# The passage from the output projection to the squared-ReLU MLP: who forms the second column pair's sums, and which product comes when

## The chip, the cores and the metric

The kernel runs on one core of one Trainium2 chip (eight cores on two dies; the other seven are idle here). The metric is the device time of one execution in microseconds, the median of several runs. A profile of one execution stands beside it; its times are counted from the first instruction.

## The reference, cut to what matters

A prompt of 256 rows and a sample of 1024 rows, 1024 wide, go through one encoder layer in fp32: two attention branches, merged by gates, an output projection with a residual, then an RMSNorm and a squared-ReLU MLP with hidden width 4096, and a last RMSNorm. The end of the layer and the encoder are all that this change concerns:

```python
    x = x + merged @ w_out
    h = _rmsnorm(x, g_mlp)
    return x + jnp.square(jax.nn.relu(h @ w_up)) @ w_down
```

## The kernel before, in words

Each fp32 matmul is done as three products of a rounded high part and a residual low part: ScalarE makes the high part (`activation` Copy into fp32r), VectorE the low part by a subtraction (`split`, L184; `split_steps`, L308). `six` (L340) then issues low weight by high activation, high weight by low activation, high by high, for each of four or eight 128-deep slices.

`h @ w_up` and the product with `w_down` are done by Strassen's method in the form with seven products. The activations `h` of the sample (transposed) are cut in four blocks: A11 and A12 come from rows 0 to 511, A21 and A22 from rows 512 to 1023. Seven left factors are held split in SBUF for the whole of `h @ w_up`: A11, A12, A22 and the sums S1 = A21 + A22, S2 = S1 - A11, S3 = A11 - A21, S4 = A12 - S2. The raw sums are formed by VectorE in `combine` (L1361, in pieces, as a generator of twelve steps) and `combine_last` (L1379), and `halves` (L314) splits one factor in two halves of 128x1024.

The weights are taken 256 columns at a time, 16 pairs. `right_pair` (L367) is a generator: it issues the two loads of 512 KB on SyncE's queue, has GpSimd form the right sums `ta` and `tb` (four subtractions 128x512, L377 to L380), and then splits raw[0], ta, tb and raw[1] into `parts[0]` to `parts[3]`, one ScalarE and one VectorE step each. All these tiles take one of ten "w" buffers; activations take one of 33 "m" buffers. The first pair is prepared during the output projection.

`up(j, b, parts, hooks)` (L1693) does one pair. On TensorE, in order: A11 by parts[0] into a bank `x`, A12 by parts[0] into `y`, (for j > 0 the prompt's product with parts[0]), S2 by parts[1] added to `x`, S3 by parts[1] into `z`, S1 by parts[2] added to `x`, A22 by parts[2] added to `z`, S4 by parts[3] added to `x`, (for j = 0 the prompt's product with parts[0]), the prompt's product with parts[3]. One such product of the sample, `seven` (L357), is 12 matmuls of 512 columns; one of the prompt, `prompt` (L360), is 24 of 256 columns. Copies of `x` and `z` (`c1`, `c2`, `c7`, by ScalarE) are added by VectorE to later states of the banks (`relu2_sum`, L1689), which also squares the ReLU. The four blocks of the result are joined with the prompt's to `u` (128x640), GpSimd forms the four sums that the next Strassen product needs (L1743 to L1746), and SyncE's queue stores seven blocks of 320 KB (L1748). Every stage buffer (`u0` to `u6`, `c1`, `c2`, `c7`) exists once.

PSUM has eight banks under four tags: "mm" three, "sc" two, "pt" two, "pv" one. A new tile of a tag waits until an old one of the tag has been read.

From the second half of the output projection on (L1416) the order on each engine is the order of the program text (`manual_schedule` for all engines). Work of the passage is threaded into the first pair by `hooks`: `entering` (L1752) is a generator, and each `next(hooks)` in `up` issues its next piece. In the kernel before, the pieces after the successive products of the first pair are: splits of S3; the transposes of the last prompt row block (`turn_prompt(9)`, two banks "pt", copied out by ScalarE) and splits of S1; splits of A22; `combine_last` with the splits of S4; nothing; `split_prompt` (the prompt's activations, two halves). The generator `nb` of the next pair is moved by `steps_of(nb, 3)` (L1733) and by `steps_of(b, 2)` in the next call of `up`.

Of the kernel before, what the change touches and what calls it, by code (L numbers as in the profile page):

```python
# [11 lines left out]
F32R = mybir.dt.float32r  # L12
# [3 lines left out]
P = 128  # L16
# [81 lines left out]
def encoder_kernel(  # L98
# [229 lines left out]
    def turned(t, tags=("pt", "pt")):  # L328

        banks = []  # L330
        for h in range(2):
            ps = bank(tags[h], "tr")
            for i in range(4):
                k = 4 * h + i
                nc.tensor.transpose(ps[:, P * i : P * (i + 1)], xn[t][:, P * k : P * (k + 1)], ident)
            banks.append(ps.rearrange("p (i q) -> p i q", i=4))
        del xn[t]
        return banks
# [991 lines left out]
    hp_raw = {}  # L1330
    raws_h = {}

    def turn_prompt(t):

        if not hp_raw:
            for i in range(2):
                hp_raw[i] = slot("praw", (P, 4, NP))
        cols = slice(P * (t - 8), P * (t - 7))
        banks = turned(t)
        yield  # L1340
        for h in range(2):
            nc.scalar.activation(hp_raw[h][:, :, cols], banks[h], AF.Copy)
# [33 lines left out]

    combined = {}

    def combine_last():  # L1379
        s2, a12 = combined[S2], combined[S4]  # L1380
        for i in range(2):
            nc.vector.tensor_tensor(a12[i], a12[i], s2[i], op=ALU.subtract)
            act[S4][i] = slot("chi", (P, 2, 512), F32R), slot("clo", (P, 2, 512), F32R)
            split(*act[S4][i], a12[i])

    def right_up(j, out, make=wslot):
        return right_pair([w_up3[:, :, c : c + P] for c in (2 * P * j, 2 * P * j + P)], out, make)
# [1 line left out]
    with ExitStack() as pre:  # L1389
        late = pre.enter_context(tc.tile_pool(name="late", bufs=4))  # L1390

        def lslot(name, shape=(P, D), dt=F32):
            return late.tile(list(shape), dt, name=name, tag="l4", bufs=6)

        for i in (4, 5, 6):
            specs[n_out + i] = specs[n_out + i][:2] + (lslot,)
        gm = slot("gm2")
        nc.sync.dma_start(gm, g_mlp[0].partition_broadcast(P))
        xn = {}
        p0 = []  # L1400
        b0 = right_up(0, p0, slot)

        def ahead():

            yield from b0
            yield from halves(A11, raws_h[0, 0])
            yield from halves(A12, raws_h[0, 1])

        more, sums = ahead(), combine()
        for hh in range(2):  # L1410
            sl = slice(512 * hh, 512 * hh + 512)
            ws = [weight(0) for _ in range(4)]
            parts = {}
            if hh:

                ctx.enter_context(tc.manual_schedule(engines=ALL))  # L1416

            def part(t):
                if t >= NT:
                    return  # L1420
                n = 2 if hh else KC
                mhi = [qslot("mhi", (P, n, P), F32R) if hh else slot("mhi", (P, n, P), F32R) for _ in range(KC // n)]
                mlo = slot("mlo", (P, KC, P), F32R)
                for c in range(0, KC, 2):
                    split(mhi[c // n][:, c % n : c % n + 2, :], mlo[:, c : c + 2, :], mT.at(c, P * t, P, 2))
                parts[t] = [(mhi[k // n][:, k % n, :], mlo[:, k, :]) for k in range(KC)]

            part(0)
            part(1)
            for t in range(NT):  # L1430
                m = parts.pop(t)
                ps = bank("mm")
                run(mm3(ps, [(m[k], (ws[k // 2][0][:, k % 2, :], ws[k // 2][1][:, k % 2, :]))
                             for k in range(KC)]))
                if hh == 0:
                    nc.vector.tensor_tensor(x2[t][:, sl], x2[t][:, sl], ps, op=ALU.add)
                    part(t + 2)
                    if 2 <= t < 6:
                        prepare()
                    elif t in (6, 7):  # L1440
                        next(more)
                    continue
                turning = (turn_sample if t < 9 else turn_prompt)(t - 1) if t else iter(())
                next(turning, None)
                nc.vector.tensor_tensor(x2[t][:, sl], x2[t][:, sl], ps, op=ALU.add)
                xn[t] = slot("xn", (P, D))
                ss = small.tile([P, 1], F32, name="ss")
                nc.scalar.activation(xn[t], x2[t], AF.Square, accum_out=ss)
                sd = small.tile([P, 1], F32, name="sd")
                nc.scalar.activation(sd, ss, AF.Sqrt, bias=eps, scale=1.0 / D)  # L1450
                if 0 < t < 7:
                    next(more)
                steps_of(sums, (0, 1, 4)[max(t - 7, 0)])
                rs = small.tile([P, 1], F32, name="rs")
                nc.vector.reciprocal(rs, sd)
                nc.vector.scalar_tensor_tensor(xn[t], x2[t], rs, gm, op0=ALU.mult, op1=ALU.mult)
                nc.sync.dma_start(scr_x[t], x2[t])
                next(turning, None)
                part(t + 2)
                steps_of(more, (1, 1, 1, 1, 1, 3, 2, 0, 0, 0)[t])  # L1460
                steps_of(sums, (2, 3)[t - 7] if 6 < t < 9 else 0)
        run(halves(S2, combined[S2]))
        run(sums)
    narrow.close()


# [212 lines left out]
    with ExitStack() as pre:  # L1679
# [9 lines left out]
        def relu2_sum(out, ps, other):  # L1689
            nc.vector.tensor_tensor(out, ps, other, op=ALU.add)  # L1690
            nc.vector.scalar_tensor_tensor(out, out, 0.0, out, op0=ALU.max, op1=ALU.mult)

        def up(j, b, parts, hooks):  # L1693

            def prompt_out(ps, dst):
                for i, d in enumerate(dst):
                    relu2(d[:, 512:], ps[:, P * i : P * i + P])

            u = [stage(f"u{i}", TH) for i in range(7)]
            u11, u12, u22, u21 = u[A11], u[A12], u[A22], u[S3]  # L1700
            x, y, z = bank("mm", "x"), bank("pt", "y"), bank("sc", "z")
            nb = np_ = None
            seven(x, A11, parts[0], 0, last=False)
            c1 = stage("c1", 512)
            nc.scalar.activation(c1, x, AF.Copy)
            steps_of(b, 2)
            next(hooks, None)
            seven(y, A12, parts[0], 1)
            relu2_sum(u11[:, :512], y, c1)
            steps_of(b, 2)  # L1710
            if j:
                pa = prompt(parts[0])
            if j + 1 < FF // P // 2:
                np_ = []
                nb = right_up(j + 1, np_)
                next(nb)
            next(hooks, None)
            seven(x, S2, parts[1], 0, False, False)
            c2 = stage("c2", 512)
            nc.scalar.activation(c2, x, AF.Copy)  # L1720
            if j:
                prompt_out(pa, (u11, u21))
            steps_of(b, 2)
            next(hooks, None)
            seven(z, S3, parts[1], 1, last=False)
            c7 = stage("c7", 512)
            nc.scalar.activation(c7, z, AF.Copy)
            next(hooks, None)
            seven(x, S1, parts[2], 0, False, False)
            relu2_sum(u22[:, :512], x, c7)  # L1730
            next(hooks, None)
            if nb:
                steps_of(nb, 3)  # L1733
            seven(z, A22, parts[2], 1, False)
            relu2_sum(u21[:, :512], z, c2)
            next(hooks, None)
            seven(x, S4, parts[3], 1, False)
            relu2(u12[:, :512], x)
            next(hooks, None)
            if not j:  # L1740
                prompt_out(prompt(parts[0]), (u11, u21))
            prompt_out(prompt(parts[3]), (u12, u22))
            nc.gpsimd.tensor_tensor(u[S1], u21, u22, op=ALU.add)  # L1743
            nc.gpsimd.tensor_tensor(u[S2], u[S1], u11, op=ALU.subtract)
            nc.gpsimd.tensor_tensor(u[S3], u11, u21, op=ALU.subtract)
            nc.gpsimd.tensor_tensor(u[S4], u12, u[S2], op=ALU.subtract)  # L1746
            for i in (A11, S1, A22, S2, S3, A12, S4):
                nc.sync.dma_start(scr_u[j // 4][:, i, j % 4, :], u[i])  # L1748
            next(hooks, None)
            return nb, np_  # L1750

        def entering():  # L1752

            run(halves(S3, combined[S3]))
            yield
            run(turn_prompt(9))
            run(halves(S1, combined[S1]))
            yield
            run(halves(A22, combined[A22]))
            yield  # L1760
            combine_last()
            yield
            yield
            split_prompt()
            yield
# [32 lines left out]
```

## Time and profile before

| | |
|---|---|
| time, median of 3 runs | 1791.44 us (1791.1 to 1794.48) |
| span of the profiled execution | 1788.8 us |
| TensorE busy | 1731.5 us, 97% of the span |
| VectorE, ScalarE, GpSimd busy | 55%, 40%, 28% |
| granted TensorE clock, mean | 0.987 |
| output projection, second half, ends | at about 982 us |
| first pair's first product starts | at 982.66 us |
| third pair's first product starts | at 1048.50 us |

A row of the timeline gives start, duration, engine, line and operation, output and inputs; a bracket at its end is the time for which the engine stood idle before it and the instruction that, by the profile, released it. Where an instruction waited for several things, the name in the bracket can be that of another instruction of the same engine than the one that was really waited for. A matmul's duration includes its way through the array, so the rate is read from start to start. PE is TensorE, DVE VectorE, ACT ScalarE, POOL GpSimd, SPq SyncE's queue of DMA issues.

### The profile page before, as it was taken

The numbers are of one execution on the slowest core, as the hardware profiler recorded it, in microseconds if no ns is written. First come the engines' busy times: TensorE is split into PE (matmuls) and PEld (weight loads), VectorE is DVE, ScalarE is ACT, GpSimd is POOL, SyncE is SP. The second block draws the span as 40 slices with busy tenths as digits, with TensorE's granted clock in tenths as the row PEclk, the third lists the DMA queues.
The fourth block names the chain that finished last, engine by engine and source line by source line (L and its number), as shares of the span: only waits on it lengthen the run. The fifth ranks groups of instructions, "written<-read, shape, count | busy, mean of one in ns | idle before, by whom it ended". The sixth has DMA issues, their size and how long they took to land.

```text
span 1788.8 us, 25229 instructions
## 1 busy us (share of the span) xinstructions
PE 1731.5 (97%) x9248; PEld 1466.8 (82%) x9248; DVE 991.7 (55%) x1683; ACT 714.1 (40%) x1531; POOL 501.6 (28%) x396
## 2 busy tenths in 40 slices
PE   7999999999999999999999799999999999999998
PEld 6898888777777889878888688888888788888886
DVE  6623333345545466566737655454554876667575
ACT  6232223344444355454426533333333433333345
POOL 0222321223322111100010255565555451315050
PEclk9999999989999999999999899999999999999999
DMA  6415335555455853164411144433444854623333
GB/s 230 144 37 165 108 105 147 143 147 146 138 161 143 252 158 103 61 241 142 190 47 82 54 140 150 148 118 121 140 150 169 299 199 142 241 95 117 127 113 118
DMA packets 218067, 256.26 MB, mean 143 GB/s; under 512 B 21455, under 2 KB 148771, under 8 KB 217816
## 3 DMA queue, kind: packets, MB, share of 16 engines
q1 hardware_dynamic: 209512, 232.32, 40.4%
q0 software_dynamic: 7344, 20.24, 3.4%
q10 hardware_dynamic: 1088, 2.10, 0.3%
q8 instruction: 73, 1.20, 0.3%
q14 instruction: 50, 0.41, 0.1%
HBM read 169.10 MB, written 90.73 MB: 145 GB/s over the span
## 4 chain that ended last, share of the span: by engine, by line
PE 61%; DVE 3%; ACT 2%; DMA 2%; issue 1%; POOL 0%; SPq 0%; ACTq 0%; DVEq 0%; POOLq 0%
PE dn L344 20%; PE mm L192 13%; PE x L344 10%; PE pv L344 5%; PE z L344 5%; PE y L344 2%; PE pv L1053 2%; PE pt L1039 1%; PE sc L1016 1%; PE sc L1017 1%; PE mm L344 1%; DMA raw<-in_w_down_dram 0%; DVE ulo L186 0%; PE pv L538 0%; DMA raw<-in_w_in_dram 0%
## 5 line engine op out<-in xcount | busy, mean ns | idle before, releaser
L344 PE MATMUL x<-chi,wlo 128*128 128x512 f32 x424 | 172.1, 406 | 6.9 <-ACT phi L185 6.9
L344 PE MATMUL dn<-dhi,ulo 128*128 128x512 f32 x448 | 174.6, 390 | 2.8 <-DVE ulo L186 2.8
L344 PE MATMUL dn<-dhi,uhi 128*128 128x512 f32 x448 | 174.3, 389 | 0.0
L344 PE MATMUL dn<-dlo,uhi 128*128 128x512 f32 x448 | 174.3, 389 | 0.0
L344 PE MATMUL x<-clo,whi 128*128 128x512 f32 x424 | 168.5, 397 | 0.0
L344 PE MATMUL x<-chi,whi 128*128 128x512 f32 x424 | 167.9, 396 | 0.0
L377 POOL TENSOR_TENSOR tb<-raw 128x512 f32<-128x512 f32 x30 | 39.0, 1302 | 453.6 <-PE mm L192 139.6
L311 DVE TENSOR_TENSOR wlo<-ta,whi 128x1024 fp32r<-128x1024 f32 x30 | 56.6, 1887 | 184.7 <-ACT whi L309 184.7
L311 DVE TENSOR_TENSOR wlo<-raw,whi 128x1024 fp32r<-128x1024 f32 x60 | 92.4, 1540 | 105.7 <-ACT whi L309 105.7
L344 PEld LDWEIGHTS dn<-dhi,ulo 128*128 128x128 f32 x448 | 84.1, 188 | 21.4 <-DVE ulo L186 3.8
L344 PEld LDWEIGHTS x<-chi,wlo 128*128 128x128 f32 x424 | 81.8, 193 | 22.9 <-ACT phi L185 7.3
L186 DVE TENSOR_TENSOR ulo<-uraw,uhi 128x1024 fp32r<-128x1024 f32 x56 | 92.0, 1664 | 11.7 <-ACT uhi L185 11.7
L344 PEld LDWEIGHTS dn<-dlo,uhi 128*128 128x128 f32 x448 | 84.1, 188 | 17.4
L344 PEld LDWEIGHTS dn<-dhi,uhi 128*128 128x128 f32 x448 | 84.1, 188 | 17.4
L344 PEld LDWEIGHTS x<-chi,whi 128*128 128x128 f32 x424 | 81.4, 192 | 17.9
L515 ACT ACTIVATE s<-s,o 128x128 f32<-128x128 f32 (+1 forms) x120 | 52.4, 437 | 103.8 <-DVE o L513 55.2
L344 PEld LDWEIGHTS x<-clo,whi 128*128 128x128 f32 x424 | 81.9, 193 | 14.5
L1515 POOL TENSOR_TENSOR t<-raw,t 128x1024 f32<-128x1024 f32 x16 | 47.1, 2959 | 143.3 <-DMA raw<-in_w_down_dram 143.3
L1666 DVE TENSOR_TENSOR v<-v,dn 128x512 f32<-128x512 f32 x90 | 59.6, 683 | 42.6 <-PE dn L344 38.5
L344 PE MATMUL dn<-dhi,up 128*128 128x512 f32 x224 | 73.5, 389 | 0.0
L344 PE MATMUL pv<-phi,wlo 128*128 128x256 f32 x256 | 72.4, 283 | 0.9 <-ACT u L1686 0.9
L344 PE MATMUL z<-chi,wlo 128*128 128x512 f32 x184 | 72.7, 395 | 0.0
(326 smaller groups left out, 4753.0 us busy)
## 6 DMA issues: line engine op xcount, KB each, us to landing
scr_u<-u SPq DMA_DIRECT2D x112, 320.0 KB
uraw<-scr_u SPq DMA_DIRECT2D x56, 512.0 KB
raw<-in_w_in_dram SPq DMA_DIRECT2D x33, 512.0 KB
raw<-in_w_up_dram SPq DMA_DIRECT2D x32, 512.0 KB
raw<-in_w_down_dram SPq DMA_DIRECT2D x28, 512.0 KB
sg<-scr_g SPq DMA_DIRECT2D x32, 256.0 KB
uraw<-scr_u SPq DMA_DIRECT2D x28, 256.0 KB
v<-scr_v SPq DMA_DIRECT2D x96, 64.0 KB
```

Source lines behind the costliest of these rows:

```text
L186: nc.vector.tensor_tensor(lo, src, hi.bitcast(F32), op=ALU.subtract)
L192: nc.tensor.matmul(ps, a, b, start=i == 0, stop=i == len(seq) - 1)
L311: nc.vector.tensor_tensor(lo, src, hi.bitcast(F32), op=ALU.subtract)
L344: nc.tensor.matmul(ps, a, b, start=first and i == 0, stop=last and i == len(seq) - 1, skip_group_check=True)
L377: nc.gpsimd.tensor_tensor(tb[:, 0], b12, b11, op=ALU.subtract)
L515: nc.scalar.activation(s[:, h, :W], s[:, h, :W], AF.Exp, bias=nm[:, h : h + 1], accum_out=l[:, h : h + 1])
L1016: nc.tensor.matmul(ps[:, :W], q, st["k"][1][:, P * lo : P * lo + W], start=True, stop=False)
L1017: nc.tensor.matmul(ps[:, :W], q, st["k"][0][:, P * lo : P * lo + W], start=False, stop=True)
L1039: nc.tensor.transpose(ps[:, P * (i % 4) : P * (i % 4) + P], s[:, h, P * b : P * b + P], ident)
L1053: nc.tensor.matmul(pv[:, HD * h : HD * h + HD], pt[:, 2 * b + h, :], src, start=b == 0, stop=b == W // P - 1)
L1515: nc.gpsimd.tensor_tensor(o, a, b, op=ALU.subtract)
L1666: nc.vector.tensor_tensor(v, v, ps, op=ALU.add)
```

## The change

In the call for the first pair (j = 0):

- the bank `y` comes from "sc" instead of "pt";
- the second pair's right sums come from a new generator `second_pair`, where VectorE forms `ta` and `tb`, and raw[0] is split before them (in the order raw[0], sums, ta, the last sum and tb, raw[1]);
- after the first pair's product A22, a new function `first_two` does the second pair's products A11 and A12 (banks "mm" and "pt", copy in the buffer "c7"), ahead of the first pair's last product S4; the second call of `up` takes them over and begins with the prompt's product;
- VectorE's sums of `y` and `z` (`u11`, `u21`) of the first pair come after `first_two`;
- the prompt's product with parts[3] goes to a bank "mm" instead of "pv";
- the four joins of `u` are made by VectorE instead of GpSimd.

In `entering`, the splits of S1 move one piece later, and S4's difference is made in two halves: the first right behind the transposes of the last prompt block, the second, with both splits of S4, after the product A22. At the end of the output projection the last two steps of `combine` come before the splits of S2. In the call for j = 1, `u11`'s sum comes after `c2`. Pairs from the third on are as before.

```diff
-    def combine_last():
+    def combine_last(i):
         s2, a12 = combined[S2], combined[S4]
+        nc.vector.tensor_tensor(a12[i], a12[i], s2[i], op=ALU.subtract)
+
+    def second_pair(out):
+
+        raw = [wslot("raw", (P, KC, P)) for _ in range(2)]
         for i in range(2):
-            nc.vector.tensor_tensor(a12[i], a12[i], s2[i], op=ALU.subtract)
-            act[S4][i] = slot("chi", (P, 2, 512), F32R), slot("clo", (P, 2, 512), F32R)
-            split(*act[S4][i], a12[i])
+            nc.sync.dma_start(raw[i], w_up3[:, :, P * (2 + i) : P * (3 + i)])
+        yield
+
+        def parts(src):
+            out.append((wslot("whi", src.shape, F32R), wslot("wlo", src.shape, F32R)))
+            return split_steps(*out[-1], src)
+
+        yield from parts(raw[0])
+        b11, b21, b12, b22 = raw[0][:, :4], raw[0][:, 4:], raw[1][:, :4], raw[1][:, 4:]
+        ta, tb = wslot("ta", (P, 2, 4, P)), wslot("tb", (P, 2, 4, P))
+        nc.vector.tensor_tensor(tb[:, 0], b12, b11, op=ALU.subtract)
+        nc.vector.tensor_tensor(ta[:, 1], b22, b12, op=ALU.subtract)
+        nc.vector.tensor_tensor(ta[:, 0], b22, tb[:, 0], op=ALU.subtract)
+        yield
+        yield from parts(ta)
+        nc.vector.tensor_tensor(tb[:, 1], b21, ta[:, 0], op=ALU.subtract)
+        yield from parts(tb)
+        yield from parts(raw[1])
...
+        run(sums)
         run(halves(S2, combined[S2]))
-        run(sums)
...
+        def first_two(j, parts):
+
+            x, y = bank("mm", "x"), bank("pt", "y")
+            seven(x, A11, parts[0], 0, last=False)
+            c1 = stage("c7", 512)
+            nc.scalar.activation(c1, x, AF.Copy)
+            seven(y, A12, parts[0], 1)
+            opened[j] = x, y, c1
...
-            x, y, z = bank("mm", "x"), bank("pt", "y"), bank("sc", "z")
...
+            if j == 1:
+                x, y, c1 = opened.pop(j)
+                z = bank("sc", "z")
+            else:
+                x, y, z = bank("mm", "x"), bank("pt" if j else "sc", "y"), bank("sc", "z")
...
+            if j > 1:
+                relu2_sum(u11[:, :512], y, c1)
...
-                nb = right_up(j + 1, np_)
+                nb = right_up(j + 1, np_) if j else second_pair(np_)
...
             nc.scalar.activation(c2, x, AF.Copy)
+            if j == 1:
+                relu2_sum(u11[:, :512], y, c1)
...
             seven(x, S1, parts[2], 0, False, False)
+            if not j:
+                steps_of(nb, 2)
             relu2_sum(u22[:, :512], x, c7)
             next(hooks, None)
-            if nb:
+            if j and nb:
                 steps_of(nb, 3)
             seven(z, A22, parts[2], 1, False)
-            relu2_sum(u21[:, :512], z, c2)
+            if j:
+                relu2_sum(u21[:, :512], z, c2)
             next(hooks, None)
+            if not j:
+                first_two(1, np_)
+                next(hooks, None)
+                relu2_sum(u11[:, :512], y, c1)
+                relu2_sum(u21[:, :512], z, c2)
             seven(x, S4, parts[3], 1, False)
             relu2(u12[:, :512], x)
             next(hooks, None)
             if not j:
+                steps_of(nb, 1)
                 prompt_out(prompt(parts[0]), (u11, u21))
-            prompt_out(prompt(parts[3]), (u12, u22))
-            nc.gpsimd.tensor_tensor(u[S1], u21, u22, op=ALU.add)
-            nc.gpsimd.tensor_tensor(u[S2], u[S1], u11, op=ALU.subtract)
-            nc.gpsimd.tensor_tensor(u[S3], u11, u21, op=ALU.subtract)
-            nc.gpsimd.tensor_tensor(u[S4], u12, u[S2], op=ALU.subtract)
+                steps_of(nb, 2)
+            prompt_out(prompt(parts[3], "pv" if j else "mm"), (u12, u22))
+            join = nc.gpsimd if j else nc.vector
+            join.tensor_tensor(u[S1], u21, u22, op=ALU.add)
+            join.tensor_tensor(u[S2], u[S1], u11, op=ALU.subtract)
+            join.tensor_tensor(u[S3], u11, u21, op=ALU.subtract)
+            join.tensor_tensor(u[S4], u12, u[S2], op=ALU.subtract)
...
             run(turn_prompt(9))
+            combine_last(0)
+            yield
             run(halves(S1, combined[S1]))
             yield
             run(halves(A22, combined[A22]))
             yield
-            combine_last()
-            yield
+            yield
+            combine_last(1)
+            run(halves(S4, combined[S4]))
             yield
             split_prompt()
             yield
```

More of the change, by code (lines that the diff above doesn't have):

```diff
@@ L1331, in encoder_kernel, with turn_prompt @@
     raws_h = {}
-    def turn_prompt(t):
+    def turn_prompt(t, tags=("pt", "pt")):
         if not hp_raw:
@@ L1338, in turn_prompt @@
         cols = slice(P * (t - 8), P * (t - 7))
-        banks = turned(t)
+        banks = turned(t, tags)
         yield
@@ L1691, in relu2_sum @@
             nc.vector.scalar_tensor_tensor(out, out, 0.0, out, op0=ALU.max, op1=ALU.mult)
+        opened = {}
+        def first_two(j, parts):
[5 more added lines that the diff above has]
+            opened[j] = x, y, c1
         def up(j, b, parts, hooks):
@@ L1700, in up @@
             u11, u12, u22, u21 = u[A11], u[A12], u[A22], u[S3]
-            x, y, z = bank("mm", "x"), bank("pt", "y"), bank("sc", "z")
             nb = np_ = None
[L1703 to L1709, printed above, removed]
+            if j == 1:
[3 more added lines that the diff above has]
+                x, y, z = bank("mm", "x"), bank("pt" if j else "sc", "y"), bank("sc", "z")
+                seven(x, A11, parts[0], 0, last=False)
+                c1 = stage("c1", 512)
+                nc.scalar.activation(c1, x, AF.Copy)
+                steps_of(b, 2)
+                next(hooks, None)
+                seven(y, A12, parts[0], 1)
+            if j > 1:
+                relu2_sum(u11[:, :512], y, c1)
             steps_of(b, 2)
@@ L1729, in up @@
             seven(x, S1, parts[2], 0, False, False)
+            if not j:
+                steps_of(nb, 2)
             relu2_sum(u22[:, :512], x, c7)
             next(hooks, None)
-            if nb:
+            if j and nb:
                 steps_of(nb, 3)
             seven(z, A22, parts[2], 1, False)
-            relu2_sum(u21[:, :512], z, c2)
+            if j:
+                relu2_sum(u21[:, :512], z, c2)
             next(hooks, None)
+            if not j:
+                first_two(1, np_)
+                next(hooks, None)
+                relu2_sum(u11[:, :512], y, c1)
+                relu2_sum(u21[:, :512], z, c2)
             seven(x, S4, parts[3], 1, False)
```

## Prediction

> **What bounds the kernel now.** I read the page first, then the busy time by stage, then TensorE's timeline in the one stage that falls out, then the chain of work behind it, then the other engines there.
>
> ```profile
> span 1788.8 us, 25229 instructions
> PE 1731.5 (97%) x9248; PEld 1466.8 (82%) x9248; DVE 991.7 (55%) x1683; ACT 714.1 (40%) x1531; POOL 501.6 (28%) x396
> ```
>
> TensorE is the bound: whatever lets it work without a pause shortens the span one for one, and nothing else does. The change touches only the passage into the MLP, so the question is what TensorE loses there.
>
> ```profile
> 981.00:1016.80 35.80, 25.68 (x107) 20.44 (x106) 30.14 (x33) 17.82 (x23) 8.40 (x4) 0.86 0.16 45
> ```
>
> In these 35.8 us TensorE is busy for 25.68, at a granted clock of 0.86 (the number before the last two), while VectorE works for 30.14. The timeline of TensorE shows where:
>
> ```profile
> 981.87 1.04 PE L335 MATMUL tr<-ident,xn 128*128 128x128 f32 x8
> 982.66 0.47 PE L344 MATMUL x<-chi,wlo 128*128 128x512 f32 x1
> ...
> 985.28 0.39 PE L344 MATMUL x<-chi,whi 128*128 128x512 f32 x1
> 985.68 0.50 PE L344 MATMUL y<-chi,wlo 128*128 128x512 f32 x1
> ...
> 988.56 0.60 PE L335 MATMUL tr<-ident,xn 128*128 128x128 f32 x4
> 992.36 1.11 PE L335 MATMUL tr<-ident,xn 128*128 128x128 f32 x4 [3.20 <-ACT praw L1342]
> 993.13 0.78 PE L344 MATMUL x<-chi,wlo 128*128 128x512 f32 x1
> ...
> 996.94 0.39 PE L344 MATMUL z<-chi,wlo 128*128 128x512 f32 x1
> ...
> 1004.87 0.39 PE L344 MATMUL z<-chi,whi 128*128 128x512 f32 x1
> 1012.17 0.77 PE L344 MATMUL x<-chi,wlo 128*128 128x512 f32 x1 [6.91 <-ACT phi L185]
> ...
> 1016.64 0.28 PE L344 MATMUL pv<-phi,wlo 128*128 128x256 f32 x1
> ...
> 1020.53 0.38 PE L344 MATMUL pv<-phi,wlo 128*128 128x256 f32 x1 [0.87 <-ACT u L1686]
> ```
>
> Three pauses: 3.20 us between the two halves of the last transposes, 6.91 us ahead of S4, 0.87 us ahead of the prompt's second product; `y` also starts about 0.17 us late (985.68, where 985.28 + 0.23 was due). After the long two the clock is halved for a while: S2 takes 996.94 - 993.13 = 3.81 us and S4 1016.64 - 1012.17 = 4.47 us. What such a product takes otherwise is in the chain:
>
> ```profile
> 1023.66 2.75 PE x L344 x12
> 1026.41 2.72 PE y L344 x12
> 1029.13 2.87 PE pv L344 x24
> ...
> 1045.63 2.87 PE pv L344 x24
> 1048.50 2.75 PE x L344 x12
> ```
>
> So 2.72 us for one of the sample (2.75 behind a prompt's), 2.87 for one of the prompt. From 1016.80 on the chain is TensorE's, but for the short pause, and the third pair's first product starts at 1048.50. From there the code is as before: a shift of that point is the whole result, if no new wait appears.
>
> Who holds TensorE up:
>
> ```profile
> 991.73 0.58 ACT L1342 ACTIVATE praw<-tr 128x512 f32<-128x512 f32 x1
> ...
> 1002.10 2.31 DVE L1382 TENSOR_TENSOR hraw<-hraw,s 128x1024 f32<-128x1024 f32 x1
> ...
> 1010.20 1.23 DVE L186 TENSOR_TENSOR clo<-hraw,chi 128x1024 fp32r<-128x1024 f32 x1 [1.18 <-ACT chi L185]
> 1011.34 0.69 DVE L1690 TENSOR_TENSOR u<-x,c 128x512 f32<-128x512 f32 x1
> ```
>
> First pause: `y` holds one of the two "pt" banks, so the second half of the transposes waits for the copy at 991.73 to end. Second pause: S4 adds to `x`, and VectorE reads `x` only behind S4's differences and splits; it ends at 1012.03 and TensorE starts 0.14 later (the bracket's name is another instruction of ScalarE). VectorE is slow there, too: the difference takes 2.31 us, the split of the same width 1.23. It runs beside GpSimd:
>
> ```profile
> 999.45 1.64 POOL L377 TENSOR_TENSOR tb<-raw 128x512 f32<-128x512 f32 x1 [90.75 <-PE z L344]
> 1001.05 2.26 POOL L378 TENSOR_TENSOR ta<-raw 128x512 f32<-128x512 f32 x1
> ```
>
> **The change, part by part.** I lay TensorE's new order end to end, at full rate, and then look for each product at whether its inputs are there.
>
> The old way from the end of the first product (985.51) to 1048.50 is 62.99 us. The new one: `y` 2.88 (985.68 to 988.56), eight transposes 0.79 (981.87 to 982.66), seven products S2, S3, S1, A22, the second pair's A11 and A12, S4 at 2.72 = 19.04, three prompt products 8.61, five of the second pair 2.75 + 4 x 2.72 = 13.63, its last prompt product 2.87: 47.82 us. If nothing waits, 15.17 us are gained. The same from the other side: the pauses are 0.17 + 3.20 + 6.91 + 0.87 = 11.15, the slow clock 1.09 in S2, 1.75 in S4 and about 0.4 in the transposes, together 14.4; the rest are matmul tails that overhang the pauses' edges.
>
> TensorE's starts then are, on the clock of the profile: `y` 985.51, transposes 988.39, S2 989.18, S3 991.90, S1 994.62, A22 997.34, second pair's A11 1000.06, A12 1002.78, S4 1005.50, prompt 1008.2, 1011.1, 1014.0, S2 1016.8, S3 1019.6, S1 1022.3, A22 1025.0, S4 1027.7.
>
> Bank of `y`, last steps of `combine` first. `y` in "sc" finds a bank at once, and both "pt" banks are free for the transposes. The two steps (0.76 us) move ahead of the splits of S2:
>
> ```profile
> 987.09 2.36 DVE L311 TENSOR_TENSOR clo<-s,chi 128x1024 fp32r<-128x1024 f32 x2 [0.44 <-ACT chi L309]
> 989.37 0.76 DVE L1374 TENSOR_TENSOR hraw<-hraw 128x256 f32<-128x256 f32 x2
> ...
> 997.14 0.60 ACT L1720 ACTIVATE c<-x 128x512 f32<-128x512 f32 x1 [1.14 <-PE x L344]
> 997.63 2.00 ACT L309 ACTIVATE chi<-hraw 128x1024 fp32r<-128x1024 f32 x2
> ```
>
> They fill VectorE's idle time from 986.66 to 987.09 and delay S2's second residual by 0.3, to 989.7; TensorE needs it in the second half of S2, at 990.8. ScalarE no longer waits 1.33 us for them before S3's splits.
>
> From here a link of ScalarE and VectorE runs beside TensorE: copy of the last bank (0.5), two high parts (2.00), two residuals (2.36) one step behind. The residual is first read by a product's second matmul, 0.23 after its start. S3: residuals at 990.8 and 992.0, needed at 992.1 and 993.5. S1: S2's end is copied at 992.10 to 992.60, the first high part ends at 993.65, its residual at 994.92, TensorE sees it 0.14 later at 995.06 and wants it at 994.85: a wait of 0.2. A22: the same link behind S3, residual seen at 997.81, wanted at 997.78: 0.03. Second pair's A11: the high part of raw[0] follows A22's on ScalarE (to 998.3), the residual follows on VectorE (to 999.97), seen at 1000.1 for 1000.3: none, or 0.05. These three have almost no margin; I charge 0.3 in all, and 0.4 more for the scatter of such rows. Below zero they cannot go.
>
> S4: the first difference now lies behind the transposes with GpSimd idle, so 1.23 instead of 2.31; then residuals of S1 and A22, raw[0], `u22` (so `x` is read by 1000.6), second difference to 1002.4, S4's residuals at 1003.6 and 1004.8. Wanted at 1005.8 and later: margin 2. The two early products are the cover; without them S4 would stand 5.44 earlier and wait again.
>
> Prompt's activations: high parts to 1006, residuals to 1007.4, wanted at 1008.2. VectorE next: `u11`, `u21` (2.7 us), three right sums (0.6 each) to 1011.8; ScalarE's and VectorE's split of `ta` to 1014.8, wanted at 1016.8. The prompt's product with parts[3] has its own bank: the 0.87 goes.
>
> ```profile
> 1024.90 1.57 POOL L1743 TENSOR_TENSOR u<-u,u 128x640 f32<-128x640 f32 x1 [16.97 <-ACT u L1687]
> ...
> L1687 ACT ACTIVATE u<-u 128x128 f32<-128x128 f32 x7 | 2.2, 311 | 0.2
> L1686 ACT ACTIVATE u<-pv 128x128 f32<-128x128 f32 x7 | 1.9, 269 | 6.0 <-PE pv L344 6.0
> ```
>
> Joins on VectorE: 128x640 has no row there; between 0.69 (512) and 1.23 (1024) by width, an estimate of 0.82, nearer the 0.69, against GpSimd's 1.57. They start when ScalarE has put the prompt's four pieces in place (about 1.1 us, to 1015.5) and end at 1018.6. Queued behind them are the last right sum (to 1019.2) and, over ScalarE, `tb`'s residual, at 1021.6; the second pair's S1 wants it at 1022.3. Margin 0.7; with GpSimd's price for the joins (3.1 more in all) it would be 2.4 us too late, the upper end.
>
> SyncE's queue: seven stores of `u`, then the third pair's loads, in both kernels.
>
> ```profile
> 1020.34 12.22 SPq L1748 DMA_DIRECT2D scr_u<-u  x7
> 1032.65 1.18 SPq L373 DMA_DIRECT2D raw<-in_w_up_dram  x2
> ...
> 1021.00:1022.00 1.00, 1.00 (x11) 1.00 (x10) 0.00 (x0) 0.00 (x0) 0.00 (x0) 1.00 0.80 317
> 1028.00:1029.00 1.00, 1.00 (x6) 0.81 (x6) 0.98 (x1) 0.94 (x1) 1.00 (x2) 1.00 0.99 384
> ...
> 1039.01 1.29 POOL L377 TENSOR_TENSOR tb<-raw 128x512 f32<-128x512 f32 x1 [6.80 <-DMA raw<-in_w_up_dram]
> ```
>
> With the joins done by 1018.6 the loads are issued at about 1020 and the third pair starts at 1033.5: 13.5 us, where before it was 1048.50 - 1032.65 = 15.85. The load needs 6.4 (to 1039.01) and raw[0]'s split at most 3.4 more: hidden.
>
> Sum: 15.17 - 0.3 - 0.4 = 14.5 us off the profiled 1788.8 us, so a span of 1774.3. The median lies 2.64 above the span (1791.44 - 1788.8), which I carry over: 1776.9 us.
>
> **The rivals.**
>
> *A hand-over without margin opens.* The likeliest place is the second pair's A11: it needs both parts of raw[0], which take two of the ten "w" buffers, and the kernel before shows that these are full: GpSimd's first sum waited for S3 by parts[1] to end (row at 999.45). If they come free only with parts[2], at A22's end, split and residual (1.05 + 1.23 + 0.2) follow it: 2.5 us on TensorE, gain 12, 1779.4. Against it: the program asks for them right after S1, when parts[1] is free. Would such a pause halve the clock as well? In the rows 3.20 us were enough, and the loss behind them was 1.1 to 1.75 us, so up to 1781.2. The Trainium skill (TensorE: Matmul & The Clock Gate, Part 1) has the clock drop after an idle window of about 3.4 us; by it a pause of 2.5 us would keep the full clock and the first figure would hold, though the trace has it drop after 3.20 already. Chance 0.1.
>
> *A store in the way.* ScalarE's writing of the second pair's prompt part into `u21` waits for the store of the old S3 block. Behind it in ScalarE's queue are raw[1]'s high part and `c7`, and A22 waits for `c7`. To be in time ScalarE must begin on `u21` by 1022.7. Stores move at about 1 us each (317 and 384 GB/s in the rows, 320 KB), four go out together from 1016.4, so the S3 block lands at about 1021.3. At twice that, 1025, it costs 2.4 us: 1779.3. Chance 0.05.
>
> *Slower: VectorE becomes the bound.* From 987.3 to 1021.6 it has seventeen 1024-wide operations (1.14 apart), three pairs of `u` sums, four right sums and four joins: 19.4 + 4.1 + 2.4 + 3.0 = 28.9 us of 34.3, and TensorE follows it hand to mouth. At the price of the row at 1002.10, 2.31 for 1.23, they would take 54 us, S1 of the second pair would start at about 1042, 19.5 late, and the time would be 1796, slower. It decides from a factor of 1.7 on: (1022.3 + 15.2 - 987.3) / 28.9. For it: VectorE takes over the work of an engine that was there for it. Against it: that price is seen only beside GpSimd's sums, which the change removes from this stretch, and away from them a split runs at 1.23 (row at 1010.20). The Trainium skill (SBUF — State Buffer, Who interferes with whom) says that a VectorE instruction with two SBUF inputs contends with a GpSimd one that reads SBUF, the later blocking fully; in the rows both lengthen (2.31, and 2.26 for the sum beside it), but either way an idle GpSimd leaves this rival little. Chance 0.03.
>
> *No gain.* The tags or buffers put the old waits back elsewhere, within 3.6 us of 1791.44. Each pause has a cause that the diff removes, so 0.02.
>
> **How the numbers follow.** Forecast 0.8, rivals 0.1, 0.05, 0.03, 0.02. The forecast's own range is 1775.9 (all 15.17, and the 0.34 by which the lowest run lay below the median) to 1779 (joins or hand-overs 2 us worse). The range goes on through the first two rivals to 1781.5. Two per mille of the time, 3.6 us, is about what a measurement can tell from no change: faster 0.95, same 0.02, slower 0.03.
>
> **What would show it.** TensorE's timeline after 982 should hold no pause over 0.5 us, its clock in that stage should be 1.00, S4 should follow the second pair's A12 without a bracket, GpSimd should be idle until the third pair's loads land, VectorE's join rows should read about 0.82, and the third pair's first product should start near 1034. A pause ahead of the second pair's A11, A22 or S1 names the rival at work; a start near 1034 with a span over 1776 would mean that later stages gave it back, which nothing above foresees.

## The result, and the profile after

The changed kernel takes 1776.01 us (median of 4 runs, 1773.78 to 1777.76), the kernel before 1791.27 in the runs beside it (4 runs): ratio 0.9912, 95% interval 0.9895 to 0.9928. The profiled execution reads 1777.01 us with a span of 1774.8. Put on the median from which the forecast was made, 0.9912 x 1791.44 = 1775.7 us, which is 0.2 us under the lower end of the range (the median as read, 1776.01, lies 0.1 us inside it); the direction and the size (15.3 us by the medians, 14.5 forecast) are as foretold.

The stage that fell out before, from the page of busy time by stage, first two columns start to end and length, then TensorE's busy time, the clock third from the end:

```profile
981.00:1016.80 35.80, 35.80 (x195) 30.71 (x194) 31.79 (x39) 22.29 (x35) 0.00 (x0) 1.00 0.19 54
```

TensorE is busy for 35.80 of 35.80 us at a clock of 1.00, where it had 25.68 at 0.86; GpSimd does nothing. The chain of work has only TensorE in it from the transposes on (start, length, what; lines after L1378 have moved by the new code, L1710 is the sum that was L1690):

```profile
982.93 0.88 PE tr L335 x8
983.81 2.76 PE x L344 x12
986.57 2.73 PE y L344 x12
989.30 0.87 PE tr L335 x8
990.17 2.77 PE x L344 x12
992.94 2.72 PE z L344 x12
995.66 3.01 PE x L344 x12
998.66 2.72 PE z L344 x12
1001.38 2.72 PE x L344 x12
1004.10 2.72 PE y L344 x12
1006.82 2.72 PE x L344 x12
1009.54 2.87 PE pv L344 x24
1012.42 2.88 PE mm L344 x24
1015.30 2.88 PE pv L344 x24
1018.18 2.75 PE x L344 x12
```

The order is the new one: behind A22 (998.66) come the second pair's A11 and A12, then S4 at 1006.82. All lengths are those of full clock but one: S1 has 3.01 for 2.72. That is the one wait left, for a residual of S1:

```profile
995.50 0.39 PE L344 MATMUL x<-chi,wlo 128*128 128x512 f32 x1
995.84 0.50 PE L344 MATMUL x<-clo,whi 128*128 128x512 f32 x1
```

The second matmul stands 0.34 behind the first, not 0.23. On VectorE:

```profile
992.66 1.22 DVE L1381 TENSOR_TENSOR hraw<-hraw,s 128x1024 f32<-128x1024 f32 x1
994.55 2.36 DVE L311 TENSOR_TENSOR clo<-s,chi 128x1024 fp32r<-128x1024 f32 x2 [0.67 <-ACT chi L309]
...
1016.49 0.83 DVE L1792 TENSOR_TENSOR u<-u,u 128x640 f32<-128x640 f32 x1 [0.71 <-ACT u L1707]
```

S4's first difference takes 1.22 where it took 2.31, S1's first residual ends 1.2 after 994.55, just behind the time at which it is wanted, and a join takes 0.83.

The time from the first pair's first matmul to the third pair's first, called the passage here, measures the change by itself. Both starts are read from TensorE's timeline, "behind" is the rest of the span:

```
kernel               starts   passage   behind    span
before               982.66    65.68    740.46   1788.8
changed              983.56    50.96    740.28   1774.8
```

The passage is 14.72 us shorter. (The expectations below give 65.84 and 50.87. The chain states a step's start 0.16 to 0.25 us later than the timeline; 65.84 runs from a start of the timeline to one of the chain, 50.87 between two of the chain, so that their difference, 14.97, is 0.25 too large.)

### The profile page after: what moved, and what is told of

Same layout as the page of the kernel before. It is cut to its first block, busy times and chain, and to the rows that moved or that the text cites. A ratio compares the mean times of both kernels' runs of the same rounds, so it can differ in the third digit from the quotient of the medians.

```text
span 1774.8 us, 25217 instructions
## 1 busy us (share of the span) xinstructions
PE 1728.2 (97%) x9248; PEld 1465.2 (83%) x9248; DVE 991.6 (56%) x1691; ACT 712.8 (40%) x1531; POOL 484.1 (27%) x388
## 4 chain that ended last, share of the span: by engine, by line
PE 64%; DVE 2%; issue 1%; DMA 1%; ACT 1%; SPq 0%; DVEq 0%; ACTq 0%
PE dn L344 20%; PE mm L192 14%; PE x L344 11%; PE z L344 5%; PE pv L344 5%; PE y L344 3%; PE pv L1053 2%; PE pt L1039 1%; PE mm L344 1%; PE sc L1016 1%; PE sc L1017 1%; PE tr L335 0%; DVE ulo L186 0%; PE pv L538 0%; DMA raw<-in_w_in_dram 0%
## 5 line engine op out<-in xcount | busy, mean ns | idle before, releaser
L344 PE MATMUL z<-chi,whi 128*128 128x512 f32 x184 | 71.7, 390 | 0.0
```

The source lines that it names most:

```text
L344: nc.tensor.matmul(ps, a, b, start=first and i == 0, stop=last and i == len(seq) - 1, skip_group_check=True)
```

## The experiments

Each undoes one part of the change, or does one part alone, unless said otherwise.

**The changed kernel once more**, with more runs.

> The changed kernel once more, with more rounds. The passage is the time from the first pair's first product to the third pair's first product: 65.84 us before, 50.87 in the first profile of the changed kernel, so 14.97 less. Theory (the gain is TensorE's pauses and the slow clock behind them, at most 15.17 us, and what the medians showed beyond that is scatter of stages that did not change): the passage is 50.9 within 0.2 again, the ratio over five rounds comes out at 0.9915 to 0.9920 (15.0 us of 1791 is 0.9916), and the start of the passage moves by 1 us or more from profile to profile. Rival (something outside the passage got faster too): the ratio stays at or below 0.9912 with an interval that leaves out 0.9916, and the rest of the span, before or behind the passage, is shorter than in the kernel before by 0.5 us or more in each profile.

Ratio 0.9917, interval 0.9903 to 0.9932 (1775.89 against 1790.7 us); passage 50.90, and it began at 981.17, so 2.4 us earlier than in the first profile; behind it 740.33. The theory holds: the gain is the passage. All profiles of this study, with the parts of the program ahead of the passage's first matmul the same in each but for the order of VectorE's last steps:

```
kernel               starts   passage   behind    span
before               982.66    65.68    740.46   1788.8
changed              983.56    50.96    740.28   1774.8
changed, again       981.17    50.90    740.33   1772.4
y in pt              983.36    53.35    740.59   1777.3
two behind S4        982.85    55.33    740.32   1778.5
GpSimd busy          981.12    61.95    741.03   1784.1
prompt in pv         985.17    53.20    740.23   1778.6
sums on GpSimd       980.31    52.43    740.46   1773.2
joins on GpSimd      982.26    51.36    740.38   1774.0
difference whole     983.33    50.90    740.47   1774.7
combine steps last   983.51    51.68    740.61   1775.8
before, y in sc      982.25    65.95    740.40   1788.6
before, VectorE sums 984.48    66.55    740.57   1791.6
```

The rest behind the passage is the same within 0.4 us (0.8 with the loaded GpSimd); what comes ahead of it varies by 4.9 us from one execution to the next. Effects of a few us are therefore read from the passage, not from single times. Each passage but the changed kernel's was profiled once. Where a pause halves the clock, a slow stretch of 3.41 us (see the last section) costs up to 1.7 us, an estimate: half of its length. How much of it falls on work can change from one execution to the next, so smaller differences between kernels with such pauses are not shown.

**y in "pt" again.**

```diff
-                x, y, z = bank("mm", "x"), bank("pt" if j else "sc", "y"), bank("sc", "z")
+                x, y, z = bank("mm", "x"), bank("pt", "y"), bank("sc", "z")
```

> The changed kernel with the first pair's y back in a bank of pt. Theory (each edit closes its own wait, as large as the lists of ready times say): the second half of the transposes waits for the copy of the first half, which ScalarE ends about 1.85 us after the first half is through (copies at 991.14 behind S3's high parts, against a first half done at 989.9), so the passage is 2.0 us longer, 52.9, if the clock holds, and up to 3.5 longer if a pause of 1.9 us halves it. Rival (the parts simply add up): the 3.20 us pause and its slow clock come back whole, 4.9 us, 55.8. Second rival (GpSimd beside VectorE was the trouble): no change, 50.9.

Passage 53.35, 2.4 longer (ratio to the kernel before 0.9917, 0.9899 to 0.9936, which cannot tell this from the changed kernel). TensorE's timeline:

```profile
991.71 0.66 PE L335 MATMUL tr<-ident,xn 128*128 128x128 f32 x4 [1.76 <-ACT praw L1342]
```

The pause is back, but with 1.76 us instead of 3.20, since S3's high parts, behind which the copy stands, are no longer late, and the clock stays at 1.00:

```profile
990.00:991.70 1.70, 0.00 (x0) 0.00 (x0) 1.70 (x3) 1.66 (x3) 0.00 (x0) 1.00 0.50 120
991.70:995.00 3.30, 3.29 (x17) 2.78 (x18) 2.09 (x2) 0.60 (x1) 0.00 (x0) 1.00 0.01 2
```

The theory's 2.0 is met but for 0.3 at `y`'s own start; the additive 4.9 is not.

**The second pair's first two products behind S4.**

```diff
             if not j:
-                first_two(1, np_)
                 next(hooks, None)
...
             seven(x, S4, parts[3], 1, False)
             relu2(u12[:, :512], x)
+            if not j:
+                first_two(1, np_)
```

> The changed kernel with the second pair's first two products behind S4 instead of ahead of it, all else kept. Theory: S4 starts at about 1001.4 on the clock of the changed profile, its second matmul wants the first residual at 1001.6 and gets it at about 1004.5, so TensorE pauses 2.9 us; passage 53.8 at full clock, up to 55.5 if the clock halves behind the pause. Rival (what helped was VectorE without GpSimd beside it; the order does not matter): 50.9 to 51.5. Second rival (parts add up): the old pause of 6.91 and its slow clock, 8.7 us, 59.5.

Passage 55.33, 4.4 longer; ratio to the kernel before 0.9941 (0.9925 to 0.9957). On TensorE, and by stage:

```profile
1000.74 0.47 PE L344 MATMUL x<-chi,wlo 128*128 128x512 f32 x1
1003.65 0.80 PE L344 MATMUL x<-clo,whi 128*128 128x512 f32 x1 [2.44 <-DVE clo L311]
```

```profile
1003.65:1006.25 2.60, 2.60 (x6) 2.12 (x7) 2.50 (x3) 1.96 (x2) 0.00 (x0) 0.50 0.00 0
1006.50:1009.00 2.50, 2.50 (x13) 2.02 (x12) 2.46 (x4) 1.19 (x2) 0.00 (x0) 1.00 0.00 0
```

S4 waits for its first residual, 2.7 us behind its due time, and the clock is halved for the 3 us that follow. It is the largest single part: the two products are the cover under which VectorE finishes S4.

**GpSimd loaded with work of its own.** Nineteen subtractions behind a first addition, on a buffer that nothing else reads:

```diff
+                if not j:
+                    dum = stage("dum", 512)
+                    nc.gpsimd.tensor_tensor(dum, c1, c1, op=ALU.add)
+                    for _ in range(19):
+                        nc.gpsimd.tensor_tensor(dum, dum, dum, op=ALU.subtract)
```

> The changed kernel with twenty subtractions 128x512 on GpSimd added, on a buffer of their own that nothing else uses, from the first pair's first copy on: a price for the rival in which VectorE becomes the bound. Theory (VectorE's two-input operations stretch from 1.22 to about 2.3 us beside GpSimd, and TensorE follows them): in the stretch that they cover VectorE's 1024-wide residuals read 1.6 to 2.3 us, TensorE pauses ahead of S1, A22 and the second pair's products, and the passage is 8 to 20 us longer. Rival (VectorE has slack enough): the residuals stretch but the passage is less than 2 us longer. Third possibility: the residuals do not stretch, then GpSimd was not what slowed the difference at 1002.10.

Passage 61.95, 11.0 longer; ratio 0.9976 (0.9963 to 0.9988). VectorE and GpSimd:

```profile
994.01 4.03 DVE L311 TENSOR_TENSOR clo<-s,chi 128x1024 fp32r<-128x1024 f32 x2
...
1003.91 0.68 DVE L1710 TENSOR_TENSOR u<-x,c 128x512 f32<-128x512 f32 x1
```

```profile
989.12 34.34 POOL L1745 TENSOR_TENSOR dum<-dum 128x512 f32<-128x512 f32 x19
```

Two residuals take 4.03 instead of 2.36, while a sum with one input in PSUM keeps its 0.68. VectorE's timeline shows no wait in the passage until 1022.57; TensorE pauses in S1 and ahead of the second pair's A11, in the prompt's first product and ahead of the second pair's S2, and 75% of the gain is gone. So the prediction's slower rival has a real mechanism; the changed kernel escapes it because GpSimd is idle.

**The last prompt product in "pv" again.**

```diff
-            prompt_out(prompt(parts[3], "pv" if j else "mm"), (u12, u22))
+            prompt_out(prompt(parts[3], "pv"), (u12, u22))
```

> The changed kernel with the first pair's last prompt product back in the one bank pv (passage of the changed kernel: 50.9). Theory (each edit closes its own wait, as large as the ready times say): the product waits until ScalarE has taken the one before out of the bank, about 1.2 us, and the second pair's first prompt product, which now follows at once and uses pv as well, waits the same again: passage 53.3 to 53.5, two pauses of 0.9 to 1.1 us each, the clock full. Rival (the pause of before comes back as it was): one pause, 0.9 to 1.2 us, passage 52.0. Rival (hidden): 50.9.

Passage 53.20, 2.3 longer, with two pauses of 0.87 us:

```profile
1014.89 0.38 PE L344 MATMUL pv<-phi,wlo 128*128 128x256 f32 x1 [0.87 <-ACT u L1706]
...
1018.90 0.38 PE L344 MATMUL pv<-phi,wlo 128*128 128x256 f32 x1 [0.87 <-ACT u L1706]
```

In the new order three prompt products follow one another, so one bank would cost twice what it cost before.

**The second pair's right sums on GpSimd again** (`nc.gpsimd` for `nc.vector` in the four lines of `second_pair`).

> The changed kernel with the second pair's four right sums back on GpSimd, in the same place of the order. Theory: GpSimd begins when A22 by parts[2] has ended (buffers), runs about 6 us beside VectorE's second difference and S4's splits, which stretch from 1.2 to about 2.1 us, 2 to 3 us together; S4 had a margin of about 1.3 to 2 us, so the passage is 0 to 1.0 us longer, 50.9 to 51.9. Rival (VectorE without GpSimd beside it is where the gain came from): S4's pause comes back with 3 us or more and the halved clock behind it, passage 55 or more.

Passage 52.43, 1.5 longer: more than the theory's 1.0, far from the rival's 4. On VectorE, beside GpSimd's four sums from 997.75 on:

```profile
999.51 2.31 DVE L1381 TENSOR_TENSOR hraw<-hraw,s 128x1024 f32<-128x1024 f32 x1
1001.74 4.54 DVE L311 TENSOR_TENSOR clo<-hraw,chi 128x1024 fp32r<-128x1024 f32 x2
```

Those three operations are 1.09 + 2.18 slower (4.54 against 2.36) and the square ahead of them 0.7: 4.0, not the 2 to 3 that I had expected. S4's margin takes most of it; two waits of 0.32 and 0.58 in S4 are left, too short for the clock.

**The joins on GpSimd again** (`join = nc.gpsimd`).

> The changed kernel with the first pair's four joins back on GpSimd. Theory: the last right sum no longer queues behind the joins on VectorE, so tb is ready earlier, not later; the stores and the third pair's load go out 3 to 5 us later, which has cover: passage 50.9 to 51.3. Rival (what the prediction charged as the upper end: joins at GpSimd's price hold up the second pair's S1): a pause of 2 to 3 us ahead of that S1, passage 53 to 55. Second rival (the late store of the old S3 block holds ScalarE): a pause ahead of the second pair's A22, 0.5 to 2 us.

Passage 51.36, 0.46 longer. No pause ahead of the second pair's S1; on ScalarE:

```profile
1023.05 0.28 ACT L1706 ACTIVATE u<-pv 128x128 f32<-128x128 f32 x1 [1.55 <-DMA scr_u<-u]
```

ScalarE waits 1.55 us for the store of the old S3 block, as in the prediction's second rival; `c7` comes late by about 0.3 and A22 of the second pair with it. That is what VectorE's faster joins are worth here: they send the store off earlier.

**S4's difference whole** (`combine_last(0)` moved down to `combine_last(1)`).

> The changed kernel with S4's difference undivided: both halves ahead of S4's splits, behind u22's sum. Theory: VectorE's chain to S4 grows by one operation of 1.2 us and S4 had 1.3 to 2 us left, so no pause over 0.3 us, passage 50.9 to 51.3. Rival (the halves are what brought S4 in time): a pause of about 1.2 us ahead of S4, passage 52.1.

Passage 50.90, no pause. The halves bring nothing that a run could show.

**The last steps of combine behind S2's splits again** (`run(sums)` below `run(halves(S2, ...))`).

> The changed kernel with the last two steps of combine behind S2's splits again. Theory: ScalarE waits about 1.3 us for them ahead of S3's high parts; part of it is slack, the rest reaches S1, whose residual had no margin: passage 0.4 to 0.7 us longer, 51.3 to 51.6, by a longer wait in S1. Rival (hidden whole): 50.9. Rival (on the path whole): 52.2.

Passage 51.68, 0.7 longer, just above the theory's 0.6: ScalarE waits for VectorE's steps, and S1's residual comes later.

```profile
990.77 2.01 ACT L309 ACTIVATE chi<-hraw 128x1024 fp32r<-128x1024 f32 x2 [1.33 <-DVE hraw L1374]
```

**The kernel before with `y` in "sc" alone.**

> The kernel before with one edit alone: the first pair's y in sc (passage of the kernel before: 65.7). Theory (parts are not additive: the pause ahead of S4 is set by VectorE's and ScalarE's chain, not by TensorE): the 3.20 us pause and its slow clock vanish, 4.9 us, but S4 comes only as much earlier as the chain does, because the copies out of the transposes and S1's splits start earlier and GpSimd's sums then fall upon more of VectorE's splits: passage 62.2 to 63.7, the pause ahead of S4 grows to 8 or more. Rival (additive): 60.8, pause ahead of S4 unchanged at 6.9. Rival (nothing, the chain does not move): 65.7.

Passage 65.95: no gain is shown, and the theory's 62.2 to 63.7 missed. TensorE and GpSimd:

```profile
997.60 0.50 PE L344 MATMUL x<-clo,whi 128*128 128x512 f32 x1 [0.59 <-DVE clo L311]
...
1010.93 0.77 PE L344 MATMUL x<-chi,wlo 128*128 128x512 f32 x1 [7.44 <-ACT phi L185]
```

```profile
994.19 2.28 POOL L377 TENSOR_TENSOR tb<-raw 128x512 f32<-128x512 f32 x1 [85.89 <-DVE u L1691]
```

The pause in the transposes is gone, S3 ends earlier and lets GpSimd start at 994.19, before VectorE has done S1's and A22's splits; these stretch, and three waits of 0.57 to 0.59 for residuals appear. S4 comes only 0.8 us earlier than in the kernel before, counted from the first product (28.68 against 29.51), and then runs at half clock throughout: it takes 5.26 us where it took 4.47, and the prompt's product behind it, with the pause that follows, 4.20 where it took 3.89. I had the overlap with GpSimd in the theory, but too small.

**The kernel before with VectorE forming the second pair's right sums, alone** (in the old place).

> The kernel before with one edit alone: the second pair's four right sums on VectorE, in their old place of the order. Theory: without GpSimd beside it VectorE is about 3 us earlier at S4, but the four sums (2.4 us) now stand ahead of the split of the prompt's activations, so the wait moves there: S4 about 3 us earlier, a new pause of about 2 us ahead of the first prompt product, passage 64.2 to 65.2. Rival (contention is the cause of the loss): 62.5, no new pause. Rival (VectorE only gets more to do): 65.7 or more.

Passage 66.55, 0.9 longer. S4's pause shrinks as expected, and the wait moves as expected:

```profile
1011.06 0.47 PE L344 MATMUL x<-chi,wlo 128*128 128x512 f32 x1 [3.65 <-ACT phi L185]
...
1017.82 0.38 PE L344 MATMUL pv<-plo,whi 128*128 128x256 f32 x1 [2.07 <-DVE plo L186]
```

What the theory left out is that the new pause, 2.07 us, halves the clock once more (0.50 from 1019.0 to 1022.0), so that the prompt's product gives back more than S4 had won.

## Why the prediction was right, and where it was wrong

The mechanism was right step by step. TensorE's new order, laid end to end from the rows of before, puts the third pair 50.97 us behind the first matmul (2.85 for the first product, 47.82, 0.3 for waits); 50.96 were measured. The pauses of 3.20, 6.91 and 0.87 are gone, with the halved clock behind the first two.

- The three hand-overs without margin: S1 was charged 0.2 and cost 0.28; A22 and the second pair's A11 cost nothing. The 0.4 charged for scatter in them was not needed. The full gain of 15.17 was 0.16 too large, because it mixed the timeline's start of `y` with the chain's start of the third pair; 15.01 - 0.28 = 14.73, and 14.72 were measured where 14.5 were forecast.
- S4's cover is shown: two products behind S4 instead of ahead cost 4.4 us. The halved difference, which I had counted as part of the way there, is shown to bring nothing.
- The bank of `y`, the bank "mm" and the order of `combine` are worth 2.4, 2.3 and 0.7 us in the new order.
- VectorE's right sums: worth 1.5. The prediction named the contention but priced only S4's difference with it, not the splits.
- Joins: 0.83 measured, 0.82 estimated. That GpSimd's price would make the second pair's S1 2.4 us late was wrong: on VectorE the last right sum stood behind the joins, and without them it goes ahead. The 0.46 that they are worth come from the store.
- The rivals: no hand-over opened; the store was in time; VectorE did not become the bound, and the run with a loaded GpSimd shows that it could have, at a factor of 1.7 per residual, with a loss of 11.0 us. Whether a pause of 2.5 us would halve the clock, which the first rival left open, the runs answer with yes: pauses of 2.07 to 2.44 us did. The 19.5 worked out stretched everything by 1.88; in the run the sums with an input in PSUM and all that came after the end of GpSimd's work at 1023.5 (the joins, `tb`) kept their rates.

The step that failed is the lower end of the range, in "How the numbers follow": it took the whole gain and let the median fall only 0.34 us further, the distance of the lowest run shown. That term was too small. In its place the runs showed 4.5 us: the lowest of sixteen runs of the kernel before is 1786.21, under their median of 1790.7, and the highest is 1795.37; ten of the changed kernel reach from 1773.78 to 1778.81. The three runs that I had reached from 1791.1 to 1794.48, so a spread of 3.4 us stood there to be used on both sides. The gain itself did not lead out of the range: 14.72 us off the old median are 1776.7. With more runs the ratio is 0.9917, or 1776.6 us on the old median, and the interval of the first four runs, 1772.6 to 1778.5 us, holds the forecast of 1776.9. That they came out 0.2 us under the range is scatter.

Where this scatter arises can be read from the thirteen traces. The start of the passage varies by 4.9 us, and ahead of it the clock is halved for 23.9 to 34.1 us in all, in stretches of 3.41 us; the earliest start goes with 23.9, the two latest with 34.1, though two starts in the middle have 23.9 as well. Between the same two matmuls, at about 430 and 460 us, there lie 30.12 to 30.19 us in the six profiles with two such stretches there and 28.64 to 28.72 in the seven with one. Between those at about 745 and 770 us there lie 26.43 to 26.51 with one stretch (eight profiles) and 24.94 without (five). Another 1.2 us of the spread are there by 20 us already. What decides how many stretches an execution gets, and what makes the 1.2 us, stays open.

The single parts do not add up, as far as single profiles tell. Undone one at a time they cost, against the changed kernel's 50.9, 2.4 + 4.4 + 2.3 + 1.5 + 0.46 + 0 + 0.7 = 11.8 of 14.72, and two of them done alone on the kernel before gain nothing: their passages are 0.3 and 0.9 longer, which is within what a slow stretch of the clock can change.

## What to carry to other kernels

Where one engine is the bound and the others feed it hand to mouth, lay its new order end to end and write beside each step when its input is ready; the smallest margins say what the change is worth, and this agreed within 0.3 us. A wait removed alone moves to the next late input; look for that input, and for other work of the bounding engine that is ready and can be put ahead of it. Give the forecast the spread of the runs on both sides, even if the gain has an upper limit.

## What the runs showed of the hardware

- The clock of TensorE was halved in stretches of 3.41 us, or two or three of them end to end; up to the end of the passage, all those of one profile begin whole multiples of 3.41 us apart. With the two products behind S4 the stretch is 1003.07 to 1006.48. The kernel before has one of twice the length behind its pause of 6.91 us (1008.88 to 1015.71), and with `y` in "sc" one of three times behind 7.44 us (1006.64 to 1016.88). In the passages the clock was halved after pauses of 2.07, 2.24, 2.30 and 2.44 us, and stayed whole after one of 1.76. In the 3.41 us ahead of each halving TensorE had been busy for 42% of the time or less, and for 48% in those that hold the pause of 1.76. So where a pause falls on these steps may count as well as its length; no run tested that. The Trainium skill (TensorE: Matmul & The Clock Gate, Part 1) names an idle window of about 3.4 us; these traces do not agree with it as a lower limit for a pause, while the length of a slow stretch, 3.41 us, does agree with it.
- A VectorE operation on two SBUF inputs and a GpSimd one took turns. In the kernel before:

```profile
1001.05 2.26 POOL L378 TENSOR_TENSOR ta<-raw 128x512 f32<-128x512 f32 x1
1003.28 2.27 POOL L379 TENSOR_TENSOR ta<-raw,tb 128x512 f32<-128x512 f32 x1
```

```profile
1002.10 2.31 DVE L1382 TENSOR_TENSOR hraw<-hraw,s 128x1024 f32<-128x1024 f32 x1
```

GpSimd's first ends at 1003.31, VectorE's 1.10 us later, at 1004.41, and GpSimd's next 1.14 us after that, at 1005.55. That is about what each takes when the other is idle: 1.14 for VectorE and 1.24 for GpSimd (1039.01 to 1040.25), from start to start. With GpSimd loaded, two residuals follow each other in 4.03 us instead of 2.36, and an operation with an input in PSUM keeps its 0.68. So both lengthen because each waits for the end of the other's. The Trainium skill (SBUF — State Buffer, Who interferes with whom) has the later one block until the first is done; these rows agree with it.
